# A two-layer hybrid diffusion block on one core: first queries inside the last projection block, v blocks ahead of c blocks, last output tile in smaller pieces

## The chip, the cores and the metric

The kernel runs on one core of a Trainium2 chip. The core has a matrix engine (PE, TensorE), a vector engine (DVE), a scalar engine (ACT), GpSimd (POOL) and a queue engine (SP) that issues nearly all of this kernel's transfers between the chip's memory and the core's own. The metric is the device time of one execution in microseconds (us); lower is better.

## The reference, cut to what matters

Two layers of a hybrid block over 1024 latent tokens and 256 context tokens with 1024 channels. In the second layer, the last one, the context tokens are read but not written.

```python
for l in range(DEPTH):                                  # DEPTH = 2
    h = rmsnorm(x, g) * (1.0 + scale) + shift           # x: latent tokens; the same for ctx
    xq, xk, xv, xz_a, xb, xa, xq_a, xkv_a, xz_b, xh, xbg, xcg, xz_c = split_in(h @ w_in)
    a = gated_delta(silu(conv5(xq)), silu(conv5(xk)), silu(conv5(xv)), xb, xa)   # 4 heads, both directions
    a = rmsnorm(a, gdn_norm_g) * silu(xz_a)
    q = rope(rmsnorm(xq_a) @ w_qb);  k, v = keys_values(rmsnorm(xkv_a) @ w_kvb)   # 4 heads of 64 + 32
    b = softmax(q k^T / sqrt(96)) v * silu(xz_b)
    c = xbg * conv3(xcg * xh) * silu(xz_c)
    x = x + gate * (concat(a, b, c) @ w_out)
return rmsnorm(x, final_norm_g)
```

## The kernel before, in words

Every product is done in three matmuls on a high and a low part of each operand (`mm3`, L84). A layer runs in these stages.

**Normalised inputs and latent projections.** The tokens are normalised, modulated and transposed into `h_hi`, `h_lo` (`h_c` for context). `mla_tile` projects each of the ten 128-token tiles to a row of 352 numbers, kept in the memory tensor `mla_d`: 160 for keys and values, 192 for queries.

**Input projection.** `run_blocks` walks a list `bl` of 24 blocks, each with 128 output columns. A block runs 24 matmuls with 512 columns for each of two groups of latent tokens and, where context tokens are needed, 24 with 256 columns (L452). Its weights are loaded three blocks ahead and split two ahead (ACT L75, DVE L76). After the matmuls comes `post0` (copies, convolution, gates), and `post1` (transposes on PE, L516) two blocks later, behind the first group of that block. A k, q or v block has a convolution with four taps on DVE (L466), a SiLU on ACT (L495 for v, L498 for q), ten transposes (eight for q in layer 2) and, for v, a multiplication by row (DVE L519), after which the result goes to `vr_d` (L530). A c group consists of four blocks (h, gate c, gate b, z) with two taps and three multiplications on DVE. The order in `bl` is: four k, q0, z, q1, z, q2, q3, eight c, four v, two z blocks of the attention gate (`zb_d`, L568). In layer 2 the q, c and z blocks have only 1024 tokens, the k and v blocks 1280.

**Beside the projection.** Generators ("lanes") interleave other work by planned ticks: the delta rule's decay tables and a blockwise triangular inverse on DVE (L680 and L681, 186 instructions of each, small and serial; L653 among them), then ten `merge`s (PE L720 to L755), one for each tile, whose result goes to `nn_d`. When all ten merges have been issued, `kv_lane` runs three wide over the ten tiles: it loads `mk` from `mla_d` (L824), transposes it twice on PE (L827, L828), and writes `ckv` and `pes` by ACT and DVE (L832, L833). `load_qkv` (L787 to L809), called at the last block but one, loads and splits the query and key weights `wq_r`, `wk_r` and starts `q_rows` (`mq`, L846 to L860).

**Start of attention.** After the last block, PE's order is the order of the code. `key_rope` issues eight transfers from `pes` into the key tiles `kh`, `kl` (latent) and `kc` (context) (L1060). Two `q_head` (L865 to L888) follow: five matmuls each (L84, `qa`, `qb`, `wq`), an ACT copy to `qt`, then the rotation on DVE (L883, L884), POOL (L885), ACT, POOL (L887). Then come `k_pair` (L84, `ckv`), `a_max` (L1104 on PE, L1106 on DVE), the scores, and the recurrences of the delta rule, whose operands are loaded into `ring` tiles (L1203 and L1206) and used from L1228 and L1238 on. These transfers and those of `kv_lane` are all in SP's single queue, in one order. A transfer also waits for the one eight places back on its lane (`DMAHW0` to `DMAHW7`).

**Output projection.** `finish` normalises a tile, runs 24 matmuls for each half of 512 output columns, and adds the gated result to `xt` (L1370, L1371). In the last layer the squares are summed by half (ACT L1375), and the final norm scale follows (DVE L1379, POOL L1380), then two multiplications by scale and weights (L1383) and two stores (L1384).

The functions that the change touches follow, with the line numbers of the profile.

## Time and profile before

| | before |
|---|---|
| median of 3 runs | 1713.01 us |
| lowest and highest | 1711.97 and 3195.78 us |
| the profiled execution, its own time | 1712.38 us |
| its span, first to last instruction | 1710.7 us |
| mean granted clock of PE, share of full | 0.984 |
| PE busy | 1648.7 us (96%) |
| DVE busy | 1095.8 us (64%) |
| ACT busy | 760.1 us (44%) |
| POOL busy | 632.7 us (37%) |

Busy times add up an engine's instructions. What ends a stretch is read from the waits: in a timeline an entry such as [1.29 <-ACT qt L79] says that the engine sat idle for 1.29 us before the instruction, and what released it. A repeated instruction is one row with a count, and its time then runs from the first one's start to the last one's end.

### The profile page before, as it was taken

The numbers are of one execution on the slowest core, as the hardware profiler recorded it, in microseconds if no ns is written. First come the engines' busy times: TensorE is split into PE (matmuls) and PEld (weight loads), VectorE is DVE, ScalarE is ACT, GpSimd is POOL, SyncE is SP. The second block draws the span as 40 slices with busy tenths as digits, with TensorE's granted clock in tenths as the row PEclk, the third lists the DMA queues.
The fourth block names the chain that finished last, engine by engine and source line by source line (L and its number), as shares of the span: only waits on it lengthen the run. The fifth ranks groups of instructions, "written<-read, shape, count | busy, mean of one in ns | idle before, by whom it ended". The sixth has DMA issues, their size and how long they took to land.

```text
span 1710.7 us, 29900 instructions
## 1 busy us (share of the span) xinstructions
PE 1648.7 (96%) x10964; PEld 1311.5 (77%) x10964; DVE 1095.8 (64%) x2041; ACT 760.1 (44%) x1909; POOL 632.7 (37%) x848
## 2 busy tenths in 40 slices
PE   7999999999998999998999999999999979999998
PEld 5887888787887877765788887777777768776586
DVE  2534648888355767765566345589996577766664
ACT  4744554422444543344354435544335444434432
POOL 0420334332221456557331211544222135557731
PEclk9999999999999899999999999999999989999999
DMA  9332466464145745544442313564543464555541
GB/s 359 129 127 79 156 210 226 126 206 163 59 133 144 253 160 180 184 145 148 145 142 98 120 56 114 180 206 159 191 133 110 128 214 163 161 185 161 175 157 49
DMA packets 195402, 266.54 MB, mean 156 GB/s; under 512 B 50528, under 2 KB 115248, under 8 KB 195256
## 3 DMA queue, kind: packets, MB, share of 16 engines
q1 hardware_dynamic: 195256, 264.64, 47.5%
q8 instruction: 87, 1.43, 0.3%
q14 instruction: 59, 0.48, 0.1%
HBM read 182.71 MB, written 79.17 MB: 153 GB/s over the span
## 4 chain that ended last, share of the span: by engine, by line
PE 71%; DVE 10%; DMA 7%; issue 4%; ACT 3%; POOL 3%; SPq 1%; DVEq 0%; POOLq 0%; ACTq 0%
PE bank L452 27%; PE bank L84 23%; PE bank L1161 4%; PE bank L1238 2%; PE bank L1257 2%; PE bank L1104 2%; PE bank L1251 2%; PE bank L1256 2%; DVE pr L680 2%; PE bank L1228 2%; DVE Mb L681 1%; PE bank L516 1%; DVE acc L466 1%; POOL gcb L617 1%; DMA wa<-in_w_ada_dram 1%
## 5 line engine op out<-in xcount | busy, mean ns | idle before, releaser
L452 PE MATMUL bank<-h_hi,w 128*128 128x512 f32 x1664 | 432.4, 402 | 2.4 <-DVE h_hi L283 2.4
L452 PEld LDWEIGHTS bank<-h_hi,w 128*128 128x128 f32 x1664 | 303.6, 188 | 74.6 <-issue 4.5
L452 PE MATMUL bank<-h_lo,w 128*128 128x512 f32 x832 | 216.5, 401 | 0.0
L452 PEld LDWEIGHTS bank<-h_lo,w 128*128 128x128 f32 x832 | 153.3, 188 | 37.3 <-issue 2.1
L466 DVE SCALAR_TENSOR_TENSOR acc<-pad,col,acc 128x1284 f32<-128x1284 f32 (+1 forms) x104 | 157.4, 1513 | 10.5 <-ACT acc L463 8.3
L1131 POOL TENSOR_TENSOR vt<-vt,probT 128x512 f32<-128x512 f32 x110 | 143.7, 1324 | 19.0 <-ACT probT L1145 18.1
L84 PE MATMUL bank<-wo_hi,mix 128*128 128x512 f32 x576 | 146.7, 405 | 1.6 <-ACT wo_hi L75 1.3
L1145 ACT ACTIVATE probT<-bank 128x512 f32<-128x512 f32 (+1 forms) x168 | 96.5, 590 | 98.7 <-PE bank L84 92.3
L84 PEld LDWEIGHTS bank<-wo_hi,mix 128*128 128x128 f32 x576 | 109.3, 192 | 29.0 <-ACT wo_hi L75 2.8
L76 DVE TENSOR_TENSOR w<-wr,w 128x1024 fp32r<-128x1024 f32 x52 | 65.4, 1260 | 97.5 <-ACT w L75 97.4
L1106 DVE TENSOR_REDUCE mx<-bank 128x1 f32<-128x512 f32 (+1 forms) x200 | 108.5, 584 | 10.1 <-PE bank L1104 8.9
L452 PE MATMUL bank<-h_c,w 128*128 128x256 f32 x816 | 109.1, 286 | 0.0
L452 PEld LDWEIGHTS bank<-h_c,w 128*128 128x128 f32 x816 | 101.5, 188 | 6.1 <-issue 4.1
L75 ACT ACTIVATE w<-wr 128x1024 fp32r<-128x1024 f32 x52 | 55.0, 1061 | 85.0 <-PE bank L452 66.1
L84 PE MATMUL bank<-qt,kh 97*128 97x512 f32 (+1 forms) x256 | 84.5, 411 | 3.6 <-ACT probT L1145 3.3
L1161 PE MATMUL bank<-probT,vt 128*64 128x512 f32 (+1 forms) x336 | 81.1, 605 | 0.0
L1234 POOL TENSOR_TENSOR ring<-ring,qx 128x512 f32<-128x512 f32 x32 | 41.5, 1298 | 93.4 <-DMA ring<-row_d 71.2
L681 DVE TENSOR_TENSOR Mb<-Mb,pr 128x31 f32<-128x31 f32 (+15 forms) x186 | 70.4, 379 | 5.0
L84 PE MATMUL bank<-wo_lo,mix 128*128 128x512 f32 x288 | 73.5, 395 | 0.0
L680 DVE TENSOR_TENSOR pr<-L,Mb 128x31 f32<-128x31 f32 (+15 forms) x186 | 69.7, 375 | 4.8
L617 POOL TENSOR_TENSOR gcb<-gcb,gc 128x1024 f32<-128x1024 f32 x20 | 43.6, 2184 | 67.4 <-DMA gcb<-row_d 43.0
L522 ACT ACTIVATE jk<-bank 128x128 f32<-128x128 f32 x152 | 42.1, 277 | 51.5 <-PE bank L516 29.2
(309 smaller groups left out, 3201.4 us busy)
## 6 DMA issues: line engine op xcount, KB each, us to landing
wr<-in_w_blk_dram SPq DMA_DIRECT2D x52, 512.0 KB
wa<-in_w_ada_dram SPq DMA_DIRECT2D x32, 512.0 KB
gcb<-row_d SPq DMA_DIRECT2D x20, 512.0 KB
nn_d<-N SPq DMA_DIRECT2D x20, 512.0 KB
ring<-vr_d SPq DMA_DIRECT2D x40, 256.0 KB
ring<-nn_d SPq DMA_DIRECT2D x40, 256.0 KB
qk_d<-gcb SPq DMA_DIRECT2D x18, 512.0 KB
ring<-kt_d SPq DMA_DIRECT2D x36, 256.0 KB
```

The costliest lines, as they stand in the source:

```text
L75: A.activation(out=hi, in_=raw, func=ACTF.Copy)
L76: eng.tensor_tensor(out=lo, in0=raw, in1=hi.bitcast(F32), op=ALU.subtract)
L84: T.matmul(outp, lhsT=lh, rhs=rh, start=q == 0, stop=q == n - 1)
L452: T.matmul(pb[:, 0:n], lhsT=self.w[:, wi, k, :], rhs=hg[g][hi][:, k, :], start=q + k == 0, stop=q == 2 and k == KD - 1)
L466: V.scalar_tensor_tensor(out=acc[:, 2:hi], in0=pad[:, 2 + t - r:hi + t - r], scalar=col[:, ci:ci + 1], in1=acc[:, 2:hi], op0=ALU.mult, op1 ...
L617: P.tensor_tensor(gcb, gcb, bc(gc[:, i, :], 128), ALU.subtract)
L680: V.tensor_tensor(out=pv, in0=bc(L[:, 0:k, k], w), in1=N[:, k:k + 1, k:32].to_broadcast([128, k, w]), op=ALU.mult)
L681: V.tensor_tensor(out=N[:, 0:k, k:32], in0=N[:, 0:k, k:32], in1=pv, op=ALU.subtract)
L1106: V.tensor_reduce(mx[:, gk:gk + 1], pb[:, 0:n], AX.X, ALU.max)
L1131: P.tensor_tensor(acc, a0, a1, ALU.add)
L1145: A.activation(out=pts[r][:, kk, 0:n], in_=pb, func=ACTF.Exp)
L1161: T.matmul(u["po"][64 * r:64 * r + 64, 0:n], lhsT=vx[:, kt, hh * 64:hh * 64 + 64], rhs=pts[r][:, kk, 0:n], start=kt == keys[0], stop=kt == ...
```

## The change

Three edits.

1. `load_qkv` is called one block earlier (the last block but two) and no longer splits `wq`. A new `split_qkv`, called at the last block but one, does that and starts a new lane `first_queries`: `q_rows` of the first 512 tokens, then the first two `q_head`, 1.2 planned us apart. After the projection the program no longer issues these two but waits in its plan until they have been issued.
2. The four v blocks stand ahead of the eight c blocks.
3. In the last output tile the second half of the columns is done in two pieces of 256, with 48 matmuls of 256 columns in place of 24 of 512. The final norm's weights are multiplied into `xt` before the scale is known, and the scale is applied at the end on two engines: the first half on ACT, the second on DVE.

Lines behind L800 move by 12 in the new kernel, and by more behind `finish`.

```diff
                 if q + 3 < n:
                     blocks[q + 3].load()
+                if q == n - 3:
+                    load_qkv()
                 if q == n - 2:
-                    load_qkv()
+                    split_qkv()
                 b.post0(b)
...
+        def first_queries():
+            yield from q_rows(qgs[0])
+            for h in range(2):
+                yield 1.2
+                q_head(qgs[0], h)
+
+        def split_qkv():
+            wq_r = qkv["wq_r"]
+            wq = st([128, 4, 4, 128], "W8", F32R, name="wq")
             split(wq_r[:, 0], wq[:, 0], wq[:, 1])
...
-            sch.add(q_rows(qgs[0]))
+            qkv["wq"] = wq
+            sch.add(first_queries())
...
         bl += [conv_block("q", h) for h in range(2, 4)]
+        bl += [conv_block("v", h) for h in range(4)]
         bl += [c_block(j, q) for j in range(2) for q in range(4)]
-        bl += [conv_block("v", h) for h in range(4)]
         bl += [z_block(O_ZB, j, zb_d) for j in range(2)]
...
         key_rope()
-        sch.until(lambda: qgs[0] in QA)
-        for gh in heads(units[0]):
-            q_head(*gh)
+        sch.until(lambda: (qgs[0], 1) in Q)
         for _ in k_pair(0):
             pass
...
+                w_ = 256 if last and q and i == act[-1] else 512
+                for c0 in range(0, 512, w_):
+                    mm3(pw[:, c0:c0 + w_], [(mix[:, a_, k], w[:, k, c0:c0 + w_]) for a_, w in ((0, wh), (1, wh), (0, wl)) for k in range(KD)])
...
+                        if s0 > 1:
+                            V.tensor_tensor(out=sf[:, 0:1], in0=sf[:, 0:1], in1=sf[:, 1:2], op=ALU.add)
+                        elif i == act[-1]:
+                            V.tensor_tensor(out=xt[:, cs], in0=xt[:, cs], in1=gates[1][:, cs], op=ALU.mult)
...
+            if i == act[-1]:
+                V.tensor_tensor(out=xt[:, cs], in0=xt[:, cs], in1=gates[1][:, cs], op=ALU.mult)
             P.tensor_tensor(sf[:, 0:1], sf[:, 0:1], nhalf[:, 0:1], ALU.pow)
             for q in range(2):
                 cs = slice(512 * q, 512 * q + 512)
-                V.scalar_tensor_tensor(out=xt[:, cs], in0=xt[:, cs], scalar=sf[:, 0:1], in1=gates[1][:, cs], op0=ALU.mult, op1=ALU.mult)
+                if i < act[-1]:
+                    V.scalar_tensor_tensor(out=xt[:, cs], in0=xt[:, cs], scalar=sf[:, 0:1], in1=gates[1][:, cs], op0=ALU.mult, op1=ALU.mult)
+                elif q:
+                    V.tensor_scalar(xt[:, cs], xt[:, cs], sf[:, 0:1], None, ALU.mult)
+                else:
+                    A.activation(out=xt[:, cs], in_=xt[:, cs], func=ACTF.Copy, scale=sf[:, 0:1])
                 S.dma_start(out=out[0, i * 128:(i + 1) * 128, cs], in_=xt[:, cs])
```

How the rows move, at three places.

SP's queue in layer 1, from the first of the key transfers to the last; before (`kh`, `kl`, `kc` are the key tiles, `ring` the operands of the recurrence; the names in brackets are the semaphores that a transfer waits for):

```order
L1060 DMA kl<-pes 32x2x1024 [waits DMAHW0_49]
L1203 DMA ring_5671<-vr_d 128x512 [waits DMAHW4_49,DMAHW1_49,PE_49]
L1203 DMA ring_5671<-nn_d 128x512 [waits DMAHW2_49]
L1060 DMA kc<-pes 33x2x256 [waits DMAHW3_49,PE_49,Activation_49]
L568 DMA zb_d<-zs 128x1280 [waits Activation_49]
L1060 DMA kc<-pes 32x2x256 [waits DMAHW5_49,DVE_49]
L1060 DMA kc<-pes 33x2x256 [waits DMAHW6_49]
L1060 DMA kc<-pes 32x2x256 [waits DMAHW7_49]
```

and after:

```order
L1072 DMA kl<-pes 32x2x1024 [waits DMAHW6_49,DVE_49]
L836 DMA mk<-mla_d 128x160 [waits DMAHW7_49,DMAHW1_49,PE_49]
L1072 DMA kl<-pes 32x2x1024 [waits DMAHW0_49]
L1215 DMA ring_5703<-vr_d 128x512
L1215 DMA ring_5703<-nn_d 128x512 [waits DMAHW2_49]
L1215 DMA ring_5703<-kt_d 128x512 [waits DMAHW3_49]
L1218 DMA ring_5703<-qk_d 128x512 [waits DMAHW4_49]
L568 DMA zb_d<-zs 128x1280 [waits DMAHW5_49,Activation_49]
L1072 DMA kc<-pes 33x2x256 [waits DMAHW6_49,PE_49,Activation_49]
L1072 DMA kc<-pes 32x2x256 [waits DMAHW7_49,DVE_49]
L1072 DMA kc<-pes 33x2x256 [waits DMAHW0_49]
L1072 DMA kc<-pes 32x2x256 [waits DMAHW1_49]
```

The four transfers into `kc` now stand behind four ring loads where the first of them stood behind two, and the load of the last key tile (`mk`) stands between the two transfers into `kl`.

SP's queue in layer 2, around the end of the last block; before (`mk` are the key tiles' loads, `zb_d` the store of the last block's gate):

```order
L530 DMA vr_d<-sg 128x10x128 [waits DMAHW4_49,DVE_49]
L824 DMA mk<-mla_d 128x160 [waits DMAHW5_49,PE_49]
L824 DMA mk<-mla_d 128x160 [waits DMAHW6_49,DMAHW0_49,PE_49]
L568 DMA zb_d<-zs 128x1024 [waits DMAHW7_49,Activation_49]
L1060 DMA kh<-pes 33x2x1024 [waits Activation_49,Pool_49]
L1060 DMA kc<-pes 33x2x256 [waits DMAHW1_49,PE_49,Activation_49]
L1060 DMA kl<-pes 32x2x1024 [waits DMAHW2_49,DVE_49]
L1060 DMA kc<-pes 32x2x256 [waits DMAHW3_49,DVE_49]
L1060 DMA kh<-pes 33x2x1024 [waits DMAHW4_49]
```

and after:

```order
L836 DMA mk<-mla_d 128x160 [waits DMAHW0_49,PE_49]
L836 DMA mk<-mla_d 128x160 [waits DMAHW3_49,DMAHW1_49,PE_49]
L836 DMA mk<-mla_d 128x160 [waits DMAHW4_49,DMAHW2_49,PE_49]
L568 DMA zb_d<-zs 128x1024 [waits Activation_49]
L836 DMA mk<-mla_d 128x160 [waits Pool_49]
L836 DMA mk<-mla_d 128x160 [waits DMAHW5_49,DMAHW2_49,PE_49]
L836 DMA mk<-mla_d 128x160 [waits DMAHW6_49,Pool_49]
L836 DMA mk<-mla_d 128x160 [waits DMAHW7_49,DMAHW4_49,PE_49]
L1072 DMA kh<-pes 33x2x1024 [waits DMAHW0_49,Activation_49]
L1072 DMA kh<-pes 33x2x1024 [waits DMAHW1_49]
L1072 DMA kl<-pes 32x2x1024 [waits DVE_49]
```

Four loads of key tiles have moved behind the store of the last block's gate, two of them wait for POOL, and all transfers into the key tiles are behind them.

DVE in layer 2, the rows around a convolution in the four blocks that follow the q blocks; before that is a c block (two taps):

```order
L684 COPY L<-Mb 64x1024
L685 COPY L<-Mb 64x1024
L653 TENSOR_TENSOR gcb<-bank,gcb 128x512 x2
L594 TENSOR_TENSOR pad<-bank,pad 128x512
L76 TENSOR_TENSOR w<-wr,w 128x1024
L466 SCALAR_TENSOR_TENSOR acc<-pad,col_107,acc 128x1024 x2
L669 TENSOR_TENSOR L<-Mb,bb 64x1024
L670 TENSOR_TENSOR L<-Mb,bb 64x1024
L598 TENSOR_TENSOR acc<-bank,acc 128x512
```

and after a v block (four taps, and later the multiplications L519):

```order
L681 TENSOR_TENSOR Mb<-Mb,pr 128x6x26
L466 SCALAR_TENSOR_TENSOR acc<-pad,col_107,acc 128x1284
L680 TENSOR_TENSOR pr<-L,Mb 128x135
L653 TENSOR_TENSOR gcb<-bank,gcb 128x512 x2
L466 SCALAR_TENSOR_TENSOR acc<-pad,col_107,acc 128x1284
L681 TENSOR_TENSOR Mb<-Mb,pr 128x5x27
L466 SCALAR_TENSOR_TENSOR acc<-pad,col_107,acc 128x1284
L680 TENSOR_TENSOR pr<-L,Mb 128x112
L466 SCALAR_TENSOR_TENSOR acc<-pad,col_107,acc 128x1284
L76 TENSOR_TENSOR w<-wr,w 128x1024
L681 TENSOR_TENSOR Mb<-Mb,pr 128x4x28
L519 TENSOR_TENSOR sg<-bank,rki 128x512 x2
```

The taps of a v block now stand among the rows of the triangular inverse (L680 and L681).

## Rows read from the trace of the kernel before

**Rows 1.** The page, busy time of each engine over the span.
```profile
PE 1648.7 (96%) x10964; PEld 1311.5 (77%) x10964; DVE 1095.8 (64%) x2041; ACT 760.1 (44%) x1909; POOL 632.7 (37%) x848
```

**Rows 2.** Timeline of PE, layer 1: start, duration, line, operation, [idle before].
```profile
542.02 2.08 PE L452 MATMUL bank<-h_c,w 128*128 128x256 f32 x16
...
544.07 1.20 PE L452 MATMUL bank<-h_c,w 128*128 128x256 f32 x8
...
550.65 0.50 PE L1104 MATMUL bank<-kh,qt 96*128 96x512 f32 x1 [1.29 <-ACT qt L79]
...
554.99 0.55 PE L1104 MATMUL bank<-kc,qt 96*128 96x256 f32 x1 [3.26 <-DMA kc<-pes]
```

**Rows 3.** Timeline of SP's queue, layer 1.
```profile
545.72 1.13 SPq L1203 DMA_DIRECT2D ring<-vr_d  x1
...
548.28 0.88 SPq L1060 DMA_DIRECT2D kc<-pes  x1
...
549.81 3.24 SPq L1060 DMA_DIRECT2D kc<-pes  x3
```

**Rows 4.** Timeline of PE, layer 2, end of the projection.
```profile
1364.31 1.41 PE L452 MATMUL bank<-h_hi,w 128*128 128x512 f32 x5
...
1366.93 0.30 PE L827 MATMUL bank<-cst,mk 128*128 128x128 f32 x1 [0.77 <-DMA mk<-mla_d]
...
1374.19 0.51 PE L1104 MATMUL bank<-kh,qt 96*128 96x512 f32 x1 [2.58 <-ACT qt L79]
...
1377.37 0.79 PE L1104 MATMUL bank<-kh,qt 96*128 96x512 f32 x1 [1.97 <-ACT qt L79]
...
1380.13 2.04 PE L1238 MATMUL bank<-ring 128*128 128x128 f32 x8 [0.69 <-DMA ring<-nn_d]
```

**Rows 5.** Timeline of SP's queue, layer 2.
```profile
1363.45 1.55 SPq L824 DMA_DIRECT2D mk<-mla_d  x2
1367.72 0.32 SPq L568 DMA_DIRECT2D zb_d<-zs  x1
1368.81 0.94 SPq L1060 DMA_DIRECT2D kh<-pes  x1
...
1376.06 0.67 SPq L1203 DMA_DIRECT2D ring<-vr_d  x1
```

**Rows 6.** Timeline of POOL, layer 2, the first rotation of the queries.
```profile
1372.22 1.25 POOL L885 TENSOR_TENSOR r<-r,r 32x512 f32<-32x512 f32 x1 [21.14 <-DVE r L884]
```

**Rows 7.** DVE groups: count, busy us and mean ns of one (L681, L680: page).
```profile
L466 DVE SCALAR_TENSOR_TENSOR acc<-pad,col,acc 128x1284 f32<-128x1284 f32 x84 | 131.2, 1562 | 8.7 <-ACT acc L463 6.8
L681 DVE TENSOR_TENSOR Mb<-Mb,pr 128x31 f32<-128x31 f32 (+15 forms) x186 | 70.4, 379 | 5.0
L680 DVE TENSOR_TENSOR pr<-L,Mb 128x31 f32<-128x31 f32 (+15 forms) x186 | 69.7, 375 | 4.8
```

**Rows 8.** Timelines of PE and ACT, layer 2, transposes of the last two q blocks.
```profile
1155.85 1.09 PE L516 MATMUL bank<-cst,qx 128*128 128x128 f32 x8 [3.61 <-ACT qx L498]
1165.53 1.06 ACT L498 ACTIVATE qx<-acc 128x1024 f32<-128x1024 f32 x1 [0.33 <-DVE acc L466]
1170.41 1.03 PE L516 MATMUL bank<-cst,qx 128*128 128x128 f32 x8
```

**Rows 9.** Core-wide windows, layer 2: window, PE, PEld, DVE, ACT, POOL busy, PEclk, DMA share, GB/s.
```profile
1160.00:1180.00 20.00, 20.00 (x99) 16.58 (x98) 19.27 (x39) 11.46 (x39) 8.13 (x13) 0.99 0.69 232
1380.00:1400.00 20.00, 18.59 (x105) 16.48 (x105) 14.69 (x35) 4.17 (x9) 4.11 (x4) 0.77 0.72 255
```

**Rows 10.** Timeline of all engines, the kernel's end.
```profile
1701.08 2.03 PE L84 MATMUL bank<-wo_lo,mix 128*128 128x512 f32 x8
1703.14 0.69 DVE L1370 TENSOR_TENSOR tm<-bank,gate_x 128x512 f32<-128x512 f32 x1 [4.18 <-PE bank L84]
...
1704.66 0.63 ACT L1375 ACTIVATE tm<-xt 128x512 f32<-128x512 f32 x1 [4.88 <-DVE xt L1371]
...
1706.22 1.42 DVE L1383 SCALAR_TENSOR_TENSOR xt<-xt,sf,gate_c 128x512 f32<-128x512 f32 x2 [0.66 <-POOL sf L1380]
```

More of the change, by code (lines that the diff above doesn't have):

```diff
@@ L797, in load_qkv @@
                             in_=mla_w_kvb[l].rearrange("p (h s f) -> s p h f", h=4, s=2)[w])
-            wq = st([128, 4, 4, 128], "W8", F32R, name="wq")
             for b_ in range(2):
@@ L802, in load_qkv @@
                 P.tensor_copy(out=wq_r[:, b_, :, 97:128:2], in_=wq_r[:, b_, :, 64:96:2])
+            wk = st([128, 2, 512], "P4", F32R, name="wk")
+            V.tensor_scalar(wk_r, wk_r, col[:, 77:78], None, ALU.mult)
+            split(wk_r, wk[:, 0], wk[:, 1])
+            qkv.update(wq_r=wq_r, wk=wk)
+        def first_queries():
[6 more added lines that the diff above has]
+            wq = st([128, 4, 4, 128], "W8", F32R, name="wq")
             split(wq_r[:, 0], wq[:, 0], wq[:, 1])
@@ L806, in load_qkv @@
             P.memset(wq[64:128, 3].bitcast(F32), 0.0)
-            wk = st([128, 2, 512], "P4", F32R, name="wk")
-            V.tensor_scalar(wk_r, wk_r, col[:, 77:78], None, ALU.mult)
-            split(wk_r, wk[:, 0], wk[:, 1])
-            qkv.update(wq=wq, wk=wk)
-            sch.add(q_rows(qgs[0]))
+            qkv["wq"] = wq
+            sch.add(first_queries())
         kvf = Flags()
@@ L1366, in finish @@
                 wh, wl = wo[q]
-                mm3(pw, [(mix[:, a_, k], w_[:, k]) for a_, w_ in ((0, wh), (1, wh), (0, wl)) for k in range(KD)])
-                cs = slice(512 * q, 512 * q + 512)
-                tm = st([128, 512], "P2", name="tm")
-                V.tensor_tensor(out=tm, in0=pw, in1=gates[0 if i < NX else 1][:, cs], op=ALU.mult)
-                V.tensor_tensor(out=xt[:, cs], in0=xt[:, cs], in1=tm, op=ALU.add)
-                if last:
-                    if q == 0:
-                        sf = st([128, 2], "st", name="sf")
-                    A.activation(out=tm, in_=xt[:, cs], func=ACTF.Square, scale=D ** -0.5, accum_out=sf[:, q:q + 1])
+                w_ = 256 if last and q and i == act[-1] else 512
+                for c0 in range(0, 512, w_):
+                    mm3(pw[:, c0:c0 + w_], [(mix[:, a_, k], w[:, k, c0:c0 + w_]) for a_, w in ((0, wh), (1, wh), (0, wl)) for k in range(KD)])
+                    cs = slice(512 * q + c0, 512 * q + c0 + w_)
+                    tm = st([128, 512], "P2", name="tm")
+                    V.tensor_tensor(out=tm[:, 0:w_], in0=pw[:, c0:c0 + w_], in1=gates[0 if i < NX else 1][:, cs], op=ALU.mult)
+                    V.tensor_tensor(out=xt[:, cs], in0=xt[:, cs], in1=tm[:, 0:w_], op=ALU.add)
+                    if last:
+                        if q == 0:
+                            sf = st([128, 4], "st", name="sf")
+                        s0 = q + (c0 > 0)
+                        A.activation(out=tm[:, 0:w_], in_=xt[:, cs], func=ACTF.Square, scale=D ** -0.5, accum_out=sf[:, s0:s0 + 1])
+                        if s0 > 1:
+                            V.tensor_tensor(out=sf[:, 0:1], in0=sf[:, 0:1], in1=sf[:, 1:2], op=ALU.add)
+                        elif i == act[-1]:
+                            V.tensor_tensor(out=xt[:, cs], in0=xt[:, cs], in1=gates[1][:, cs], op=ALU.mult)
             if not last:
@@ L1378, in finish @@
                 return
-            V.scalar_tensor_tensor(out=sf[:, 0:1], in0=sf[:, 0:1], scalar=EPS, in1=sf[:, 1:2], op0=ALU.add, op1=ALU.add)
+            V.scalar_tensor_tensor(out=sf[:, 0:1], in0=sf[:, 0:1], scalar=EPS, in1=sf[:, s0:s0 + 1], op0=ALU.add, op1=ALU.add)
+            if i == act[-1]:
+                V.tensor_tensor(out=xt[:, cs], in0=xt[:, cs], in1=gates[1][:, cs], op=ALU.mult)
             P.tensor_tensor(sf[:, 0:1], sf[:, 0:1], nhalf[:, 0:1], ALU.pow)
```

## The prediction, made blind

> **What bounds the kernel now.** I read the page first: PE is busy for 1648.7 of 1710.7 us [rows 1], so its own work is the bound, and a change that removes no matmul can give at most a share of the 62 us in which PE is idle. Then I read PE's waits and its timeline at the places that the change touches. At the end of layer 1's projection PE waits 1.29 us for the rotated queries and 3.26 us for the transfers into `kc` [rows 2]. At the end of layer 2's it waits 0.77 us for a key tile, 2.58 and 1.97 us for the queries and 0.69 us for a ring load [rows 4]. After its last matmuls, from about 1703.1, 7.6 us pass to the end of the span [rows 10]. That makes 18.2 us, 1.1% of the time: what the change aims at is smaller than the 2% (34 us) that a measurement of this kernel can tell from no change. The third look is at who would be late next: SP's queue, in which the transfers stand in one fixed order [rows 3, 5], and DVE, which during the triangular inverse of layer 2 is busy 19.27 of 20 us [rows 9].
>
> **Layer 1, the first queries earlier.** The two query heads leave the stretch behind the projection, so the 1.29 us for `qt` [rows 2] cannot recur. But the wait that ends last there is the one for `kc`. Before, SP issues ring loads at 545.72, the first `kc` transfer at 548.28, and the last three until 549.81 + 3.24 = 553.05 [rows 3]; PE goes on at 554.99, 1.9 us later. In the new order four ring loads stand ahead of all four `kc` transfers, two more than before. A ring load holds the queue for 1.13 us [rows 3], with its gap 1.2, so the last `kc` transfer is issued 2 x 1.2 = 2.4 us later, if the queue starts when it did. The last tile's load, now between the two `kl` transfers, can only add to it. What PE saves on queries it waits for `kc`. I take +2.4 us. From below the bound is that both waits vanish, -4.6; from above it is twice the two loads, +4.8.
>
> **Layer 2, the first queries earlier.** Before, the last matmul of the projection ends at 1364.31 + 1.41 = 1365.7 [rows 4]. Now ten query matmuls (0.254 each, from the eight in 2.03 of [rows 10]: 2.5 us) come ahead of it and three tiles' transposes move behind it (about 0.8 us, six at 0.13, the step between the last ones being half of their 0.27 [rows 4]), so it ends some 1.7 us later. The 2.58 and 1.97 us for `qt` go, and the question is again what is late next. In the new order of SP's queue four of the ten key tiles' loads stand behind `zb_d`, and the first of them also waits for POOL's addition for head 0, whose buffer it takes over. Head 0's matmuls end seven matmuls (1.8 us) ahead of the block's end; behind them come two DVE products of 0.69 (the price of a DVE step of 512 columns [rows 10]) and the addition of 1.25 [rows 6], 2.6 us alone and up to 4.2 with the tiles' evictions ahead of them on DVE. So the addition ends 0.8 to 2.4 us after the block. The eighth tile's load is issued 0.8 behind that (two take 1.55 [rows 5]) and a load is used 2.7 us after its issue: the second of the pair starts at 1363.45 + 0.78 and PE uses it at 1366.93 [rows 4, 5]. With 0.7 us for the evictions, the first `kh` transfer is issued 5.0 to 6.6 us after the block's end, where before it was 1368.81 - 1365.7 = 3.1 us [rows 5]. The eight key transfers and then the ring loads follow in the queue as before (1368.81 to 1376.06 [rows 5]). Before, PE waited at 1380.13 for just such a ring load, though only for 0.69 us. So PE's recurrences begin 1.7 + (1.9 to 3.5) = 3.6 to 5.2 us later. I take +4.0, near the lower end since DVE has fewer evictions ahead of the products than before. The bounds: -5.2, if the three waits of [rows 4] vanish, and +6 with a second look-behind in the queue.
>
> The Trainium skill (DMA: Bandwidth & Descriptors, the section on the anatomy of one DMA) gives a fit of 2.0 us plus bytes over 436 GB/s; for a key tile of 82 KB that would be 2.2 us, and this term 0.5 us less. The fit is for another issue path, and the row above shows 2.7; I go by the row.
>
> **v ahead of c.** PE's matmuls stay the same in sum; what moves is when DVE has to deliver. In layer 2 I count in the new order the DVE work from the last tap of the last q block to the last tap of the last v block: 16 taps of 1.562 = 25.0 us, 39 pairs of the inverse of 0.375 + 0.379 = 29.4 us [rows 7], and 39 others, most of them 512 wide, at 0.69 [rows 10] = 26.9 us: 81.3 us. PE's work between the two blocks' transposes is 192 matmuls of 512 columns (48.8 us at 0.254), 72 of 256 (0.13 each from [rows 2], 9.4 us), four sets of transposes and seven of small products at 1.03 [rows 8] (11.3 us) and two merges, some 1 us: 70.5 us. So DVE falls behind by 10.8 us over four blocks. Its lead at the start is 3.8 us: the last q block's SiLU ends at 1165.53 + 1.06 = 1166.6 and PE transposes it at 1170.41 without a wait [rows 8]. To that come 3.1 us, because a v block's 24 context matmuls now stand ahead of these transposes. 10.8 - 6.9 = 3.9: PE stalls about 4 us before the transposes of the last v blocks. That such a stall is real, and that nothing passes it on PE, the 3.61 us at 1155.85 show [rows 8]. In layer 1 the q, c and z blocks have context columns too, PE has some 4 us more work over these four blocks, DVE 7 pairs (5.3 us) fewer, and the lead holds: 0. I take +4.0; the bounds are 0 and four stalls of 3.61, +14.4. What is relieved, DVE at the end of the projection, had no PE wait before, so it gives nothing by itself.
>
> **The end.** Before, the chain from the last matmul is DVE 0.69 + 0.69, ACT 0.63 and its read, DVE, POOL, and two multiplications in 1.42 [rows 10]. With 256 columns the two DVE steps and the square fall to about 0.41, 0.41 and 0.38 (a fixed 0.13 plus half the rest, an estimate), -0.8 us; the two multiplications become one on ACT (0.63, as the ACT step of [rows 10]) beside one on DVE, -0.7 us. The added multiplication by the weights lies beside POOL's step. The 48 short matmuls cost 48 x 0.13 - 24 x 0.254 = +0.15. Together -1.3 us; bounds -1.8 and -0.5. The early half's multiplication (0.69) lies beside 24 matmuls; without that cover it would cost 0.7.
>
> **The sum.** +2.4 + 4.0 + 4.0 - 1.3 = +9.1 us on the profiled execution's 1712.4 gives 1721.5; the median of the runs shown is 0.6 above that execution, so I give 1722.
>
> **Rivals.**
> A: the waits for queries were the ones that counted. The key tiles' loads and the `kc` transfers then come as early against PE as before, layer 1 gains 1.3, layer 2 5.2, v stalls nothing, the end -1.3: 1712.4 - 7.8 = 1704.6. For it: the two largest waits of [rows 4] are for `qt`. Against it: right behind them PE waits for a ring load, and for `kc` in layer 1.
> B: DVE's backlog decides. If the lead of 6.9 us is not there because DVE's small serial rows stretch beside POOL, each of the four v blocks stalls like the row at 1155.85: 4 x 3.61 = 14.4, with layer 2's transition at +6 and the rest as forecast +21.5: 1734. It decides from the point at which the first v block's SiLU ends after PE has reached its transposes. The low clock that follows waits (0.77 in 1380 to 1400 [rows 9], between its levels of 1.2 and 2.4 GHz) would go with it. For it: the 19.27 of 20 us [rows 9]. Against it: q3's transposes had their 3.8 us of lead in that very stretch.
> C: nothing moves but the end, since the queue also starts earlier with the evictions: 1712.4 - 1.3 = 1711.1.
>
> **How the numbers follow.** I give the forecast 0.45, B 0.20, A 0.20, C 0.15. The range of the forecast alone, with the bounds of its terms half used, is 1714 to 1729; for 8 in 10 it goes from 1704, which takes in C and A, to 1732, which leaves out most of B. All cases lie within 2% of 1713 (1679 to 1747): 0.96 for no change that can be told. Slower by more needs B with both transitions at their upper bounds, 0.03; faster by more needs more idle time than these places hold, 0.01.
>
> **What would show it.** Right: in layer 1 no wait of `a_max` for `qt`, and one for `kc` that ends some 12 us after the projection's last matmul; in layer 2 waits for `mk` and the ring loads where those for `qt` were, the first `kh` transfer more than 5 us after the last projection matmul; PE waits for SiLU at the transposes of the last v blocks in layer 2 and none in layer 1; about 6.3 us from the last matmul to the end of the span. Wrong: `kh` issued as early as before with PE going straight into the recurrences (A), or a wait at every v block (B).

## The result, and the profile after

| | before | after |
|---|---|---|
| median | 1712.49 us (4 runs) | 1730.64 us (4 runs) |
| the profiled execution, its own time | 1712.38 us | 1728.24 us |
| its span | 1710.7 us | 1726.2 us |
| mean granted clock of PE | 0.984 | 0.980 |

The ratio is 1.0119, with a 95% interval of 1.0105 to 1.0134. One run of before that took 3195.78 us is left out of it. By this ratio the change makes the kernel slower by 20 us (18 to 23), which is less than 2% but clearly more than nothing. The forecast was 1722.

The page shows that no engine has more to do in sum: PE's busy time is that of before, and its idle time went from 62.0 to 77.2 us. So the loss is waiting, and what follows from it [rows 1 has the same line of before]:

```profile
PE 1649.0 (96%) x10988; PEld 1312.5 (76%) x10988; DVE 1096.7 (64%) x2046; ACT 761.2 (44%) x1912; POOL 631.4 (37%) x848
```

PE's waits, from the view that sums them by line and releaser (in total, times, longest):

```profile
PE bank L839 <- DMA mk<-mla_d: 8.6, 4, 4.8
...
PE bank L720 <- DVE tt L709: 3.5, 3, 2.2
...
PE bank L1116 <- ACT kr L79: 2.8, 1, 2.8
```

L839 is the transpose of a key tile (L827 before), L1116 is `a_max` (L1104 before), and L720 to L755 are the `merge`s. The wait for `qt` is gone. The waits for the key tiles (0.8 in before) and most of those at the merges (before: 1.4 at L746, 0.5 at L755) are new. Of the 3.5 us at L720, 3.2 lie in layer 1, at 354.24 and 385.76.

**The projection of layer 2.** Its first L452 starts at 997.1 and its last ends at 1380.1, so it takes 383.0 us, where before it took 369.7 (996.0 to 1365.7). PE's timeline of after, every wait from 1150 to 1262:

```profile
1157.82 1.21 PE L516 MATMUL bank<-cst,qx 128*128 128x128 f32 x8 [4.16 <-ACT qx L498]
...
1195.46 0.45 PE L720 MATMUL bank<-tt,Mm 32*32 32x32 f32 x32 [0.25 <-issue]
...
1207.56 2.12 PE L452 MATMUL bank<-h_hi,w 128*128 128x512 f32 x8 [2.86 <-DVE tt L738]
...
1215.83 0.68 PE L755 MATMUL bank<-N,tt 64*64 64x64 f32 x16 [1.61 <-issue]
...
1236.17 0.23 PE L729 MATMUL bank<-tt 32*32 32x32 f32 x4 [2.12 <-ACT tt L723]
...
1261.30 0.45 PE L720 MATMUL bank<-tt,Mm 32*32 32x32 f32 x32 [0.37 <-DVE tt L709]
```

They add up to 11.4 us. Before had one such wait, that of L516, with 3.61 [rows 8]. None of after's stands at the transposes of a v block (L516 with `acc`); those of the four v blocks begin at 1192.08, 1217.44, 1236.72 and 1254.08 without a wait. What happened at 1207.56 is to be seen in DVE's timeline of after:

```profile
1200.01 1.55 DVE L466 SCALAR_TENSOR_TENSOR acc<-pad,col,acc 128x1284 f32<-128x1284 f32 x1
...
1201.74 1.55 DVE L466 SCALAR_TENSOR_TENSOR acc<-pad,col,acc 128x1284 f32<-128x1284 f32 x1
...
1203.50 1.55 DVE L466 SCALAR_TENSOR_TENSOR acc<-pad,col,acc 128x1284 f32<-128x1284 f32 x1
...
1205.25 1.55 DVE L466 SCALAR_TENSOR_TENSOR acc<-pad,col,acc 128x1284 f32<-128x1284 f32 x1
1206.83 0.59 DVE L738 TENSOR_TENSOR tt<-bank,bco 32x128 f32<-32x128 f32 x2
```

PE had done the merge's small products (L729, L732) by 1200.4. Their eviction L738, 0.59 us for two, stands behind four taps of a v block and runs at 1206.83. Until then it holds a bank that the next group of L452 needs, and PE, which works in the order of its queue, stands still from about 1204.7 to 1207.56.

The waits at 1215.83 (for which the profile names no releaser) and 1236.17 have another way. Both products need a copy on ACT (L749, L723), and in ACT's timeline of after these copies stand behind copies into a v block's `pad`:

```profile
1214.10 1.36 ACT L79 ACTIVATE pad<-bank 128x512 f32<-128x512 f32 x3 [5.04 <-DVE pr L680]
1215.33 0.40 ACT L749 ACTIVATE tt<-bank 128x256 f32<-128x256 f32 x1
...
1234.59 1.36 ACT L79 ACTIVATE pad<-bank 128x512 f32<-128x512 f32 x3 [4.46 <-DMA vr_d<-sg]
1235.83 0.30 ACT L723 ACTIVATE tt<-bank 128x128 f32<-128x128 f32 x1
```

At 1234.59 ACT waits for a store (`vr_d<-sg`, L530): the result of an earlier v block, a tile from the same pool as `pad`, has to be in memory first. At 1214.10 the profile names DVE. So of the new waits at the merges only those at L738 and L709 (2.86 and 0.37) are for an eviction on DVE, and by these rows 3.7 us come through ACT.

The windows show the same from further off (columns as in [rows 9]): the stretch from 1140 to 1320 of before, of after, and of e1 below, in this order.

```profile
1140.00:1320.00 180.00, 175.89 (x1624) 140.47 (x1623) 153.65 (x293) 73.75 (x175) 60.64 (x107) 0.99 0.46 150
```

```profile
1140.00:1320.00 180.00, 167.27 (x1435) 135.18 (x1433) 161.72 (x298) 68.85 (x158) 57.63 (x104) 0.98 0.48 149
```

```profile
1140.00:1320.00 180.00, 165.67 (x1404) 134.28 (x1403) 156.50 (x287) 66.19 (x154) 55.44 (x103) 0.94 0.48 149
```

In after, PE is idle for 8.6 us more (175.89 - 167.27), and a clock lower by 0.01 over 180 us stands for another 1.8, an estimate from figures rounded to 0.01. With the 1.7 us that the forecast gives to the queries that moved in, that is 12.1 of the 13.3 us by which the projection grew.

**The end of layer 1's projection.** PE's and SP's timelines of after, which answer to [rows 2, 3]:

```profile
547.62 3.04 PE L452 MATMUL bank<-h_c,w 128*128 128x256 f32 x24
555.48 0.45 PE L839 MATMUL bank<-cst,mk 128*128 128x128 f32 x1 [4.83 <-DMA mk<-mla_d]
...
555.79 3.55 PE L84 MATMUL bank<-ckv,wk 128*128 128x512 f32 x9
...
562.78 0.39 PE L1116 MATMUL bank<-kc,qt 96*128 96x256 f32 x1 [0.26 <-DMA ring<-vr_d]
```

```profile
546.53 2.53 SPq L1072 DMA_DIRECT2D kh<-pes  x2
549.16 0.66 SPq L1072 DMA_DIRECT2D kl<-pes  x1
549.93 1.04 SPq L836 DMA_DIRECT2D mk<-mla_d  x1
...
556.77 3.21 SPq L1072 DMA_DIRECT2D kc<-pes  x4
```

The last key tile's load stands in SP's queue behind three key transfers and is issued at 549.93, when the block's matmuls are nearly over. PE waits 4.83 us for it, and the `kc` transfers, which need that tile, come at 556.77 (before: 548.28 and 549.81). Its place in the queue is not all: from its issue to its use 5.55 us pass (555.48 - 549.93), where [rows 4, 5] give 2.7 for another such load, and 4.32 in e2 below (549.30 - 544.98). From 549.90 to 555.50 the DMA engines are busy for 0.95 of the time. After the wait the nine products of `k_pair` take 3.55 us at a granted clock of 0.50, the lower of its two levels (1.2 of 2.4 GHz).

**The end of layer 2's projection**, answering to [rows 4, 5], PE and then SP:

```profile
1379.47 0.62 PE L452 MATMUL bank<-h_hi,w 128*128 128x512 f32 x2
...
1384.20 0.44 PE L839 MATMUL bank<-cst,mk 128*128 128x128 f32 x1 [2.93 <-DMA mk<-mla_d]
...
1394.41 0.55 PE L1116 MATMUL bank<-kc,qt 96*128 96x256 f32 x1 [2.81 <-ACT kr L79]
...
1397.64 2.05 PE L1250 MATMUL bank<-ring 128*128 128x128 f32 x8 [0.96 <-DVE mx L1118]
```

```profile
1381.71 3.50 SPq L836 DMA_DIRECT2D mk<-mla_d  x4
1386.07 1.87 SPq L1072 DMA_DIRECT2D kh<-pes  x2
```

The first `kh` transfer is issued 6.0 us after the block's end (3.1 before), and the first operand of the recurrence is used 17.5 us after it (14.4 before). The wait just ahead of that use is DVE's (`mx`, 0.96), not a ring load's; the second such product, at 1400.01, waits 0.33 for one.

**The end of the kernel**, answering to [rows 10]:

```profile
1718.38 1.12 PE L84 MATMUL bank<-wo_lo,mix 128*128 128x256 f32 x8
1719.54 0.42 DVE L1382 TENSOR_TENSOR tm<-bank,gate_x 128x256 f32<-128x256 f32 x1 [1.64 <-PE bank L84]
...
1720.52 0.42 ACT L1388 ACTIVATE tm<-xt 128x256 f32<-128x256 f32 x1 [3.15 <-DVE xt L1383]
...
1721.98 0.72 ACT L1407 ACTIVATE xt<-xt,sf 128x512 f32<-128x512 f32 x1 [0.96 <-POOL sf L1399]
```

From the last matmul's end, 1719.5, to the end of the span, 1726.2, it is 6.7 us, where before it was 7.6.

### The profile page after: what moved, and what is told of

Same layout as the page of the kernel before. It is cut to its first block, busy times and chain, and to the rows that moved or that the text cites. A ratio compares the mean times of both kernels' runs of the same rounds, so it can differ in the third digit from the quotient of the medians.

```text
span 1726.2 us, 29972 instructions
## 1 busy us (share of the span) xinstructions
PE 1649.0 (96%) x10988; PEld 1312.5 (76%) x10988; DVE 1096.7 (64%) x2046; ACT 761.2 (44%) x1912; POOL 631.4 (37%) x848
## 4 chain that ended last, share of the span: by engine, by line
PE 77%; DVE 8%; DMA 6%; issue 3%; ACT 2%; POOL 2%; SPq 1%; POOLq 0%; ACTq 0%; DVEq 0%
PE bank L452 30%; PE bank L84 23%; PE bank L1173 4%; PE bank L1250 2%; PE bank L1269 2%; PE bank L1116 2%; PE bank L1263 2%; PE bank L1268 2%; PE bank L1240 2%; DVE acc L466 2%; DVE Mb L681 1%; DVE pr L680 1%; PE bank L188 1%; PE bank L516 1%; DMA wa<-in_w_ada_dram 1%
## 5 line engine op out<-in xcount | busy, mean ns | idle before, releaser
L452 PE MATMUL bank<-h_hi,w 128*128 128x512 f32 x1664 | 434.8, 403 | 5.4 <-DVE tt L738 2.9
L452 PEld LDWEIGHTS bank<-h_hi,w 128*128 128x128 f32 x1664 | 304.8, 189 | 78.8 <-issue 8.0
L452 PE MATMUL bank<-h_lo,w 128*128 128x512 f32 x832 | 215.7, 400 | 0.0
L452 PEld LDWEIGHTS bank<-h_lo,w 128*128 128x128 f32 x832 | 153.4, 188 | 37.6 <-issue 2.1
L466 DVE SCALAR_TENSOR_TENSOR acc<-pad,col,acc 128x1284 f32<-128x1284 f32 (+1 forms) x104 | 158.1, 1520 | 10.1 <-ACT acc L463 8.7
L84 PE MATMUL bank<-wo_hi,mix 128*128 128x512 f32 (+1 forms) x592 | 146.2, 398 | 2.4 <-ACT wo_hi L75 1.2
L452 PE MATMUL bank<-h_c,w 128*128 128x256 f32 x816 | 109.7, 288 | 0.1
L452 PEld LDWEIGHTS bank<-h_c,w 128*128 128x128 f32 x816 | 103.0, 191 | 6.2 <-issue 4.1
L681 DVE TENSOR_TENSOR Mb<-Mb,pr 128x31 f32<-128x31 f32 (+15 forms) x186 | 70.8, 381 | 4.4
L84 PE MATMUL bank<-wo_lo,mix 128*128 128x512 f32 (+1 forms) x296 | 73.5, 389 | 0.0
L680 DVE TENSOR_TENSOR pr<-L,Mb 128x31 f32<-128x31 f32 (+15 forms) x186 | 69.4, 373 | 4.4
L84 PEld LDWEIGHTS bank<-wo_lo,mix 128*128 128x128 f32 x296 | 54.6, 188 | 12.8
```

What stands on the lines that cost most here:

```text
L84: T.matmul(outp, lhsT=lh, rhs=rh, start=q == 0, stop=q == n - 1)
L452: T.matmul(pb[:, 0:n], lhsT=self.w[:, wi, k, :], rhs=hg[g][hi][:, k, :], start=q + k == 0, stop=q == 2 and k == KD - 1)
L466: V.scalar_tensor_tensor(out=acc[:, 2:hi], in0=pad[:, 2 + t - r:hi + t - r], scalar=col[:, ci:ci + 1], in1=acc[:, 2:hi], op0=ALU.mult, op1 ...
L680: V.tensor_tensor(out=pv, in0=bc(L[:, 0:k, k], w), in1=N[:, k:k + 1, k:32].to_broadcast([128, k, w]), op=ALU.mult)
L681: V.tensor_tensor(out=N[:, 0:k, k:32], in0=N[:, 0:k, k:32], in1=pv, op=ALU.subtract)
```

## The experiments

The theory after the result: the loss sits in v ahead of c, because DVE has more work beside layer 2's triangular inverse than fits into the time, and the merges stand behind it; the early queries cost a few microseconds, and the end gives one. The rivals: the early queries and their place in SP's queue make the loss, or the order has a price that isn't DVE's (the five 5 KB buffers that the v blocks and the merges share, or a fixed cost of the place). The expectations number their theories anew each time. Each kernel is compared with runs of before on the same chip (medians 1710.5 to 1711.4).

**One edit at a time.** e1 is before with the order alone, e2 is after with the old order, e3 is before with the new end alone.

```diff
 e1: before
+        bl += [conv_block("v", h) for h in range(4)]
         bl += [c_block(j, q) for j in range(2) for q in range(4)]
-        bl += [conv_block("v", h) for h in range(4)]
 e2: after
-        bl += [conv_block("v", h) for h in range(4)]
         bl += [c_block(j, q) for j in range(2) for q in range(4)]
+        bl += [conv_block("v", h) for h in range(4)]
 e3: before, with the changed finish()
```

> The kernel before with one edit, the four v blocks ahead of the c blocks; queries and end as before. Theory 1 (DVE is overbooked while the triangular inverse runs, and the v taps push the merges behind PE): nearly the whole loss is here, +11 to +15 us, 1724 to 1728, with PE waits at L720, L729, L755 or at a bank behind L738, most of them in layer 2 between 1190 and 1270, and no new wait at the two ends of the projection. Theory 2 (the transfers' order behind the projection costs the time): 1711 to 1716.

> The changed kernel with one edit undone, the c blocks ahead of the v blocks again; queries early and the end in pieces as changed. Theory 1: the waits at the merges vanish and the time falls to 1709 to 1714, since the waits for qt are replaced by waits for key tiles of about the same size and the end gives 1 us. Theory 2: the time stays at 1724 or more.

> The kernel before with the end in pieces alone. Both theories: -0.9 us, 1711 to 1712.5, and from the last L84 matmul to the end of the span 6.6 to 6.8 us where before it was 7.6.

| | median (runs) | ratio to before, 95% | projection of layer 2 in the profile |
|---|---|---|---|
| e1, order alone | 1725.15 us (1723.59 to 1727.34) | 1.0076 (1.0052 to 1.0100) | 386.0 us |
| e2, queries and end | 1715.28 us (1710.95 to 1722.04) | 1.0024 (1.0007 to 1.0041) | 371.8 us |
| e3, end alone | 1710.27 us (1707.71 to 1713.15) | 0.9996 (0.9982 to 1.0011) | 370.4 us |

The order alone costs 13 us (9 to 17), and shows the waits of after at the merges, as expected (1724 to 1728). Not expected were two waits for key tiles at layer 2's end, 1.12 and 1.53 us. The queries and the end cost 4 (1 to 7), and the end alone can't be told from nothing. Together that is 17 us; the intervals of the parts, 10 to 24 together, take in the 20 of the whole. So the times don't show that one part needs another; the rows of layer 2's end do, see below. e2 came out a little above what was expected of it, e3 a little below.

Where e2 loses is told by PE's and SP's timelines of e2 in layer 1:

```profile
549.30 0.30 PE L839 MATMUL bank<-cst,mk 128*128 128x128 f32 x1 [2.64 <-DMA mk<-mla_d]
...
549.47 3.43 PE L84 MATMUL bank<-ckv,wk 128*128 128x512 f32 x9
...
557.74 0.55 PE L1116 MATMUL bank<-kc,qt 96*128 96x256 f32 x1 [3.90 <-DMA kc<-pes]
```

```profile
542.96 1.91 SPq L1072 DMA_DIRECT2D kh<-pes  x2
544.98 0.75 SPq L836 DMA_DIRECT2D mk<-mla_d  x1
...
551.59 4.33 SPq L1072 DMA_DIRECT2D kc<-pes  x4
```

In e3 the last key tile is transposed inside the block, the `kc` transfers begin at 547.18, and PE waits 1.28 us for `qt` and 2.10 for `kc`. Its nine products of `k_pair` run at full clock:

```profile
546.48 1.91 PE L84 MATMUL bank<-ckv,wk 128*128 128x512 f32 x9
```

In e2 the granted clock is 0.54 from 549.3 to 553.0, behind the wait for the key tile, and the same nine take 1.5 us more. That makes +2.64 for the tile, +1.5 for the clock, -1.28 for `qt` and +1.80 for `kc`, 4.7 us. The recurrence's first product with its state (L1240 in e2, L1228 in e3) comes 490.1 us after the start of layer 1's projection in e2 and 485.6 in e3. In layer 2 the stretch from the projection's start to that same product takes 397.0 us in e2 and 395.3 in e3. Single profiles of kernels that are alike here differ by up to 4 us in layer 1 (before itself has 489.6 where e3 has 485.6), so the medians carry the verdict.

At layer 2's end SP's timeline of e2 is not that of after:

```profile
1365.87 3.69 SPq L836 DMA_DIRECT2D mk<-mla_d  x4
1370.31 0.32 SPq L568 DMA_DIRECT2D zb_d<-zs  x1
1371.34 1.88 SPq L1072 DMA_DIRECT2D kh<-pes  x2
```

The last four loads of key tiles go out ahead of `zb_d`, and the first `kh` transfer comes 2.7 us after the block's end at 1368.6. In e3 it comes after 3.1 us, in e1 after 3.5, in after 6.0. The first operand of the recurrence is used 14.8 us after that end in e2, 14.7 in e3, 16.3 in e1 and 17.5 in after. So the queries alone don't make after's later start: v ahead of c does a part of it by itself, and the rest comes only with both. The first key tile is transposed 11.4 us ahead of the block's end in e2 and 3.4 us ahead of it in after.

**Half of the v blocks later.** e4 is after with four c blocks, four v, four c.

```diff
+        bl += [c_block(0, q) for q in range(4)]
         bl += [conv_block("v", h) for h in range(4)]
-        bl += [c_block(j, q) for j in range(2) for q in range(4)]
+        bl += [c_block(1, q) for q in range(4)]
```

> The changed kernel with the v blocks between the two c groups (four c, four v, four c). Theory 1: half of the inverse is then done before the first v taps come, so the waits at the merges shrink to a third or half: 1715 to 1722. Theory 2: 1728 or more, as the changed kernel. A third theory, that the mere place of the v transposes on PE costs the time, gives 1728 or more too, with waits at L516.

It took 1735.15 us (1731.49 to 1741.08), ratio 1.0137 (1.0105 to 1.0168): no better than after, so the theory's number was missed. Its wait has one place. PE, then POOL, of e4:

```profile
1289.30 0.65 PE L720 MATMUL bank<-tt,Mm 32*32 32x32 f32 x32 [9.56 <-DVE tt L709]
```

```profile
1285.20 0.31 POOL L706 MEMSET tt<- 128x256 f32 x1 [10.19 <-DVE acc L466]
```

A merge's tile `tt` takes over one of the buffers from a v block's convolution. POOL clears it, and SP loads it, only when the last tap has been done, and PE waits at the merge. It is the same resource, DVE beside the inverse, but the wait goes through a buffer. That raised the question whether the buffers and not DVE's time are the cause, also in after.

**DVE's taps or the buffers.** In e5 (e1) and e6 (before) the convolution of the v blocks keeps one tap of five, the one on ACT: the four on DVE, L466, are left out. In e12 (e1) two of those four are left out. e7 is e1 and e8 is before, both with six 5 KB buffers in place of five, paid for with two of the seven 2 KB ones.

```diff
 e5, e6
-                acc = conv(pad, [t * 12 + base for t in range(5)], hi)
+                acc = conv(pad, [t * 12 + base for t in range(5)] if nm != "v" else [2 * 12 + base], hi)
 e12
+                acc = conv(pad, [t * 12 + base for t in range(5)] if nm != "v" else [t * 12 + base for t in (1, 2, 3)], hi)
 e7, e8
-    BUFS = {"B16": 7, "B4": 2, "W8": 2, "T5": 5, "P4": 4, "P2": 7, "sm": 4, "h5": 2, "br": 1, "st": 8}
+    BUFS = {"B16": 7, "B4": 2, "W8": 2, "T5": 6, "P4": 4, "P2": 5, "sm": 4, "h5": 2, "br": 1, "st": 8}
```

> The kernel before with the v blocks ahead of the c blocks, and the four side taps of every v convolution left out (the convolution is its middle tap alone; 32 DVE instructions of 1.56 us fewer). Read against the same kernel without the change of order. Theory 1 (DVE's working time beside the inverse is the price): the order then costs 0 to 3 us where it cost 14. Theory 2, new since the split order was slower than the changed one (the 5 KB buffers: pad, acc and sg of the v blocks, the inverse's two tiles and the merges' tt share five, and a merge waits for one): the order still costs 6 us or more, since the v tiles take the same buffers.

> The control: the kernel before, its order kept, with the four side taps of every v convolution left out. Both theories: 1705 to 1712, as before within 6 us, since no wait of PE in the v blocks of before was for the taps.

> The kernel before with the v blocks ahead of the c blocks and six 5 KB buffers in place of five; to make room the 2 KB buffers are five in place of seven. Read against the same buffers with the old order. Theory 1 (DVE's time): the order still costs 10 to 15 us. Theory 2 (buffers): 0 to 5 us.

> The control: the kernel before in its old order, with six 5 KB buffers and five of 2 KB. Both theories give the same: slower than before by what the two missing 2 KB buffers cost, an unknown 0 to 30 us, which the comparison with the other order on these buffers takes out.

> The kernel before with the v blocks ahead of the c blocks, and two of the four side taps of every v convolution left out (16 DVE instructions of 1.56 us fewer, half of what the run without side taps left out). If PE waits for what DVE is overbooked by: the order cost 14 us with all taps and about 1 without, and half of the taps (12.5 us a layer) leaves 0 to 6, since the lead takes part of it: 1711 to 1717. If any v block at that place costs a fixed wait: 1722 or more.

| | order | median | ratio to before, 95% | PE busy, 1140 to 1320 |
|---|---|---|---|---|
| e6, no taps | c ahead of v | 1710.43 us | 1.0000 (0.9982 to 1.0017) | 175.11 us |
| e5, no taps | v ahead of c | 1711.30 us | 1.0007 (0.9993 to 1.0020) | 172.89 us |
| e12, half the taps | v ahead of c | 1712.54 us | 1.0009 (0.9995 to 1.0023) | 171.50 us |
| e8, six buffers | c ahead of v | 1722.24 us | 1.0065 (1.0044 to 1.0085) | 175.74 us |
| e7, six buffers | v ahead of c | 1738.40 us | 1.0158 (1.0136 to 1.0179) | 166.26 us |

Without the taps the order costs nothing that can be told, and without them before isn't faster: they are free where they were. Half of them gone is enough to bring the order to 1 to 2 us above before (interval -1 to 4). Layer 2's projection goes the same way in the single profiles: 370.6 us in e6, 372.2 in e5, 375.5 in e12 and 386.0 in e1. e12 still has one wait there, 3.51 us at 1197.15 for a bank that the multiplication L519 holds. So the price isn't a fixed one for each block; it grows with the taps' time on DVE, and faster than that time. Fewer taps also let a v block give its buffers back sooner, so these runs don't part DVE's queue from the buffers. The sixth buffer makes both kernels slower, by what the missing 2 KB buffers cost, and the order still costs 16 us on top (1738.40 - 1722.24). Layer 2's projection grows by 10.6 us there, against 15.6 in e1 (both between single profiles), so by these the buffers would be a third of that stretch at most. But e7 also has fewer 2 KB buffers, and it still shows PE waiting 3.72 us at 1202.78 for L723 on ACT, so the share of the buffers stays open.

**What the early queries wait for.** e9, e10 and e13 are e2, e3 and after with the eight transfers into the key tiles issued from ACT's queue in place of SP's, so that they can't stand behind ring loads. e14 is e2 with the two query heads put back behind the projection; the load of the weights and the split of `wk` stay a block earlier. The rows of the queries start at the last block but one in all these kernels, so the expectation's "the query rows stay a block earlier" is not what the edit does.

```diff
 e9, e10, e13
-                        S.dma_start(out=dst[64:64 + w, h0:h0 + 2].bitcast(F32),
+                        A.dma_start(out=dst[64:64 + w, h0:h0 + 2].bitcast(F32),
 e14
             yield from q_rows(qgs[0])
-            for h in range(2):
-                yield 1.2
-                q_head(qgs[0], h)
...
-        sch.until(lambda: (qgs[0], 1) in Q)
+        sch.until(lambda: qgs[0] in QA)
+        for gh in heads(units[0]):
+            q_head(*gh)
```

> Queries early and the end in pieces, old order of blocks, and the eight transfers into the key tiles issued from ACT's queue in place of SP's, so that they no longer stand behind ring loads and the tiles' loads no longer behind them. Read against the same kernel with all on SP (+2 to +6 against before in its runs). Theory A (SP's order is what gave the early queries' gain back): 4 to 7 us faster than that, 1705 to 1709, the waits for mk and kc in layer 1 (2.6 and 3.9 us) down to 3 us together. Theory B (the transfers' own bandwidth is the limit there): within 2 us of it, 1711 to 1716.

> The control: the end in pieces alone, queries where they were, old order, and the key transfers on ACT's queue. Theory A: the wait for kc in layer 1 shrinks by 1 to 3 us, but the wait for qt stays: 1706 to 1710. Theory B: 1709 to 1711, as with the end in pieces alone.

> The changed kernel with the key transfers on ACT's queue. Theory A: 3 to 6 us faster than the changed kernel, 1723 to 1727; theory B: 1727 to 1731. In both the waits at the merges in layer 2 stay, so it is slower than before.

> The kernel after with c blocks ahead of v blocks (as e2_no_order), and the two first query heads put back behind the projection: only the weight load and the query rows stay a block earlier. Theory 1: the two heads' matmuls and evictions in the last block delay the last key tile, and with it the kc transfers. Then the waits for qt of the kernel before are back in layer 1 and the waits for the last key tile (2.6 us in e2) and for kc (3.9 us) shrink to those of e3_tail_only (0 and 2.1 us); the first recurrence of layer 1 comes some 4 us earlier than in e2, as far behind the start of layer 1's projection as in e3 (485 to 486 us against 490), and the time is 1709 to 1712. Theory 2: it is the earlier load and split of the weights that delay the other lanes; then layer 1's first recurrence stays at 489 to 490 us behind the start of its projection, and the time at 1714 to 1717.

| | median (runs) | ratio to before, 95% |
|---|---|---|
| e9, e2 with keys from ACT | 1719.50 us (1714.61 to 1725.03) | 1.0052 (1.0037 to 1.0068) |
| e10, e3 with keys from ACT | 1726.89 us (1723.33 to 1730.66) | 1.0090 (1.0065 to 1.0114) |
| e13, after with keys from ACT | 1736.83 us (1736.43 to 1738.12) | 1.0156 (1.0137 to 1.0175) |
| e14, heads behind the projection | 1710.78 us (1707.85 to 1713.87) | 0.9996 (0.9986 to 1.0006) |

The three with the keys on ACT are all slower than their like, which no theory had: ACT stands still while the transfers wait. ACT's timeline in e9 and in e10:

```profile
551.88 8.94 ACTq L1072 DMA_DIRECT2D kc<-pes  x4
560.87 0.59 ACT L79 ACTIVATE kh<-bank 64x512 fp32r<-64x512 f32 x1 [8.40 <-DMA ring<-nn_d]
```

```profile
551.46 5.90 ACTq L1060 DMA_DIRECT2D kc<-pes  x4
```

From the first of the four to the end of the last it is 8.9 and 5.9 us, but the issuing itself is not long. e9's rows by line (shortest, median and longest in ns):

```profile
L1072 ACTq DMA_DIRECT2D kc<-pes x4: 627/754/882, 551.9 to 560.2; - x4
```

That is some 3.0 us for four. The rest is waiting: the last `kc` transfer goes out when a ring load issued by SP has landed, as the releaser of ACT's next row says, and ACT can do nothing else until then. PE then waits 9.24 us for `kh` in e9 and 10.98 and 12.08 for `qt` in e10 (the latter in layer 2). These runs don't tell what they were made for. They do show that the edit has no sign of its own: with ACT held up, the early queries gain 7.4 us (1726.89 - 1719.50), since there the wait for `qt` is the last one.

e14 tells it. Its time is that of before and of e3, as expected (1709 to 1712), and 4.5 us under e2; the two intervals just don't overlap. PE's timeline in layer 1 is that of [rows 2] again:

```profile
549.16 0.50 PE L1113 MATMUL bank<-kh,qt 96*128 96x512 f32 x1 [1.29 <-ACT qt L79]
...
552.03 0.35 PE L1113 MATMUL bank<-kc,qt 96*128 96x256 f32 x1 [1.79 <-DMA kc<-pes]
```

The `kc` transfers are back at 546.39, and the recurrence's first product with its state comes 486.8 us after the projection's start (490.1 in e2). So it is the two heads in the last block, not the earlier weights, that delay the last key tile. No kernel of these is faster than before beyond its interval.

## Why the prediction was right and wrong, point by point

The direction was right, and the time lies inside the wide range (1704 to 1732) but outside that of the forecast alone (1714 to 1729): the change was sized at +9 and is +20. The profiles of the whole change put 13.3 of their 15.5 us into layer 2's projection.

**Layer 1's queries (+2.4): right mechanism, too small.** The wait for `qt` went, and PE got nothing for it, as forecast; `a_max`'s second product with `kc`, the last of that stretch to wait, came 12.1 us after the projection (562.78 - 550.66), where "some 12" was given, though the wait there was down to 0.26 and for a ring load. But the term priced two ring loads, and of the last key tile's load it said only that it "can only add". That load is what ended last: 4.83 us in after, 2.64 in e2. And no term stood for the clock behind that wait, 1.5 us in e2 and 1.6 in after. The times show +4 to +5 for the edit in both layers (e2 less e3 and e2 less e14), and e2's rows put most of it into layer 1 (4.7, as added up above), at the upper bound of 4.8.

**Layer 2's queries (+4.0): the steps came, but not from this edit alone, and the sum is not borne out.** In after the first `kh` came 6.0 us after the block where 5.0 to 6.6 was given. The first ring operand came 3.1 us later behind the block's end, which with the forecast's 1.7 for the later end makes 4.8 where 3.6 to 5.2 was given. That is in part luck: PE waited there for ACT's `kr` (2.81) and DVE's `mx` (0.96), and in e2, which has this edit without the order, the first `kh` comes after 2.7 us and the operand is 0.1 us later than in e3. Only together with v ahead of c do the key tiles come that late. And the argument stopped at that operand. From there to the first product with the state (L1228, L1240 after) it takes 11.1 us in after (1397.64 to 1408.71) and 12.6 before (1380.13 to 1392.77), so a part was made up. In e2 against e3 layer 2 is later by under 2 us. The step that failed is that the queries alone bring this delay, and that it is passed on whole.

The Trainium skill's fit (DMA: Bandwidth & Descriptors, anatomy of one DMA), which is for another issue path, gives 2.2 us for such a key tile by my estimate, and would have made it 4.5 to 6.1 us to the first `kh`. The 6.0 measured lies in both ranges and doesn't tell it from the 2.7 of the trace; layer 1's last load, 5.55 us from issue to use, is far from both.

**v ahead of c (+4.0): the cause right, place and size wrong.** The taps' time on DVE is the cause, as e5, e6 and e12 show, though not how much of it acts through DVE's queue and how much through the buffers that the v blocks hold. The edit costs 13 us (9 to 17). The two sums were close. In after DVE takes 81.0 us from the last tap of the last q block, which ends at 1167.46, to that of the last v block, which ends at 1248.51 (81.3 was given). PE's transposes of these two blocks stand 78.8 us apart (1175.30 to 1254.08), 6.8 of them waits, so its work is 71.9 (70.5 was given). The step that failed is the subtraction "10.8 - 6.9": the lead of 6.9 us belongs to the transposes of the v blocks. Those indeed never waited, and their lead fell by 2.3 us only. The merges had no such lead. Their evictions (L709, L738) stand in DVE's queue behind the taps: at 1207.56 it was L452's next group that needed the bank, and PE can't pass an instruction that waits. Their copies on ACT stand behind copies into `pad`. PE paid the 6.8 us for them.

The other part is the clock: over the 180 us it is 0.94 in e1, against 0.99 before, and 0.05 x 180 us is 9.0 us at the full rate. With 10.2 of idle time that more than covers the 16.3 us by which e1's projection grew; how the two overlap the rows don't tell, and some 2 of the 9.0 lie ahead of the merges' waits, behind the wait of [rows 8] (1140 to 1180: 0.83 and 1.00 by 20 us, against 0.93 and 0.99). Rival B, "DVE's backlog decides", came nearest with 1734, though by another way: it put four stalls at the transposes, and none is there. Layer 1 was put at 0, and there too PE waits at two merges for L709, 3.4 us together in e1. Its projection grows by little in e1, 465.8 us against 465.2 before, but takes 470.1 in after; how much of that is the order's no run tells.

**The end (-1.3): right.** In the profile 7.6 us became 6.7, so -0.9. The steps of 256 columns took 0.42 and 0.43 where 0.41 was given. The square took 0.42 for 0.38, and the last multiplication on ACT 0.72 for 0.63. By the medians e3 can't be told from before (0.9982 to 1.0011), an interval that holds both -0.9 us and 0.

Still open is whether the two heads could stand in the last block without the loss, if the last key tile's load went ahead of the `kh` transfers in SP's queue; that was not tried.

## What to carry to other kernels

When work is moved into a stretch where one engine is already full, compare its sum there with the time it has, and then charge the excess to the waiter with the least lead, in that engine's queue and in those that it feeds, not to the moved work's own reader: here the v blocks' transposes never waited, and PE stood still 6.8 us for the merges. A wait that is removed gives only what the next one in line leaves, so price the whole queue behind it, and follow a delay to the point at which PE no longer waits. Edits that shift the same lane of work, here that of the key tiles, are to be sized together. And a transfer moved to another engine's queue takes its waits along: that engine stands still until it may go.
